# The first product of a PEER layer on 224 tokens, with the expert rows of 32 tokens gathered by index and multiplied on VectorE

## The chip, the cores and the metric

One core of a Trainium2 chip runs the whole program. The metric is the device time of one execution in microseconds. A small part lies around the span that the trace records. Engines are named as in the profile: PE is TensorE (PEld its weight loads), DVE is VectorE, ACT is ScalarE, POOL is GpSimd, SP is SyncE. SP issues the loads of the weights; POOL can issue DMAs too.

## The reference

Two blocks of two layers each work on 256 tokens of width 1024. Only the feed-forward part of the second block's two layers is touched. There every token picks 128 of 16384 experts, 16 for each of 8 heads, by a product-key search:

```python
def peer_ffn(h, w_q, sub_keys, peer_u, peer_v):
    ...
        s = jnp.einsum('thpk,pnk->thpn', q, sub_keys)          # 8 heads, 2 halves, 128 keys
        s_top, i_top = lax.top_k(s, PEER_TOPK)                 # 16 of 128 on each half
        ...
        g_top, pos = lax.top_k(cand, PEER_TOPK)                # 16 of the 256 sums
        expert = jnp.take_along_axis(cand_idx, pos, axis=-1)   # 128 * key1 + key2
        g = jax.nn.softmax(g_top, axis=-1)
        u = jnp.take(peer_u, expert, axis=0)
        act = gelu(jnp.einsum('thkd,td->thk', u, xb))
        vv = jnp.take(peer_v, expert, axis=0)
        return jnp.einsum('thk,thkd->td', g * act, vv)
```

All inputs are FP32, and `peer_u` and `peer_v` are 64 MB a layer each.

## The kernel before, in words

The kernel does not take rows. `peer(l)` runs all 16384 experts as 128 chunks of 128, for all 256 tokens, and lets the weights of a token be zero where an expert was not chosen. A chunk c holds the experts with first key c.

- **A weight block** of 128x1024 is loaded by SP into one of four buffers `raw` (512 KB), rounded by ACT to FP32R (`whi`, L177), and the rest is taken by DVE or POOL (`wlo`, L180). `whi` and `wlo` have five buffers each. `mm3` then makes one FP32 product out of three FP32R matmuls (hi by hi, hi by lo, lo by hi; L185 to L187).
- **up(c)** multiplies a block of `peer_u` by the 256 normed tokens, 8 x 3 matmuls of 256 columns into `pA`, and puts the gelu of it into the row c of `act1` or `act2`. For c below 64 the `wlo` of every third chunk runs on POOL, all others on DVE.
- **Route**: during the chunks 0 to 54 or so, DVE carries out the top-k search as a list of small steps, let in behind the chunks in order.
- **weigh(half, t0)** takes 8 tokens and 64 chunks: DVE builds one-hot matrices in FP16 (`e2`, `e0`, `e1`), 16 small matmuls make the routing weights `pG` from them, and DVE multiplies `act` by `pG` in place (L979).
- **down(c)** rounds the row c of `act` (`wr`), and multiplies it by the block c of `peer_v`, 4 x 3 matmuls of 512 columns into the accumulators `acc`.

The order of the work in a layer: up for c = 0 to 63 with the route; up for 64 to 99 with weigh(0); then 28 chunks with down(c) and up(100+c); down for 28 to 63 with weigh(1); and down for 64 to 127. Instructions are put on each engine's queue by a scheduler that follows the program, the buffers and the holds (`issue_after`); each engine then carries out its own queue strictly in order. In the places below, DVE's queue is what counts: which instruction stands ahead of which.

Of the kernel before, what the change touches and what calls it, by code (L numbers as in the profile page):

```python
# [7 lines left out]
F32 = mybir.dt.float32  # L8
# [8 lines left out]
D = 1024  # L17
# [11 lines left out]
FIRST_HI, FIRST_LO = "aaaa", "vvvv"  # L29

FREE, LAST = 4, 6

AHOLD, HOLD, PACE = 24, 10, 85
NEG = -1e30
# [2 lines left out]
def bc(ap, shape):  # L37
    return ap.to_broadcast(shape)
# [77 lines left out]
class Net:  # L116
# [776 lines left out]
        nc.scalar.copy(dst[0][:, c, :], src)  # L893
        nc.vector.tensor_tensor(dst[1][:, c, :], src, dst[0][:, c, :].bitcast(F32), op=ALU.subtract)

    def peer(self, l, norm, g2, nxt, out=None):
        nc, tc, d = self.nc, self.tc, self.d


        N1, NA, FIN, GATE, TAIL = 64, 100, 58, 110, 4  # L900
        LAG = 128 - NA
        with ExitStack() as ctx:
            P = lambda c, name, bufs=1: c.enter_context(tc.tile_pool(name=f"{name}{l}", bufs=bufs))
            h = norm.h
            wr = self.np.tile([128, 2, 2, S], F32R, tag="xa1", name="wr")
            slots = P(ctx, "pea").tile([128, 4, S], F16, name="slots")
# [6 lines left out]

            def up(c, dst, lo_eng=None):
                w = self.split_w(d["peer_u"][l, c], lo_eng=lo_eng)
                p = self.pa.tile([128, S], F32, tag="sc", name="pA")
                for k in range(KD):
                    mm = self.mm3(p, [v[:, k * 128:(k + 1) * 128] for v in w], [v[:, k, :] for v in h],
                                  k == 0, k == KD - 1)
                return mm, nc.scalar.activation(dst, p, AF.Gelu)  # L920
# [6 lines left out]
            steps, ends = self.route(rctx, l, sc, wI, wP)  # L927
            took = 0
            for c in range(64):
                mark = up(c, act1[:, c, :], nc.gpsimd if c % 3 == 0 else nc.vector)  # L930
                if c % 3:
                    with tc.issue_after(self.last_lo.ins):
                        while took < 1.7 * (c + 1):
                            took += next(steps, 1000)
                if c > FIN and self.bg:
                    if c == FIN + 1:
                        with tc.issue_after(self.last_dma.ins):
                            self.ada_setup("ab")
                    spare()
                if c == FIN:  # L940
                    with tc.issue_after(mark[0].ins), tc.issue_after(mark[1].ins):
                        for end in ends:
                            end()
            assert next(steps, None) is None
            rctx.close()
            mid = ExitStack()
# [7 lines left out]
            def weigh(hf, t0):  # L954

                pg = self.pt.tile([128, 64, 8], F32, tag="tp", name="pG")
                e2 = B.tile([128, 2, 128, 4], F16, tag="e2", name="e2")
                e0 = B.tile([128, 2, 64, 4], F16, tag="e0", name="e0")
                tg = lambda a, n: bc(a.rearrange("p (g t) -> p g t", t=4)[:, :, None, :], [128, 2, n, 4])
                i1, i2 = [wI[:, j, t0:t0 + 8] for j in range(2)]  # L960
                nc.vector.tensor_tensor(e2, bc(self.iota4[:, None], [128, 2, 128, 4]), tg(i2, 128), op=ALU.is_equal)
                nc.vector.tensor_tensor(e0, bc(self.iota4[:, None, hf * 64:hf * 64 + 64], [128, 2, 64, 4]), tg(i1, 64),
                                        op=ALU.is_equal)
                for g in range(2):
                    e1 = B.tile([128, 2, 64, 4], F16, tag="e1", name="e1", bufs=2)
                    w = wP[:, :, t0 + 4 * g:t0 + 4 * g + 4]
                    nc.vector.tensor_tensor(e1, bc(e0[:, g:g + 1], [128, 2, 64, 4]), bc(w[:, :, None, :], [128, 2, 64, 4]),
                                            op=ALU.mult)
                    for t in range(4):
                        for j in range(2):  # L970
                            nc.tensor.matmul(pg[:, :, 4 * g + t], lhsT=e2[:, g, :, t], rhs=e1[:, j, :, t],  # L971
                                             start=(j == 0), stop=(j == 1))
                rows = [(i, (hf * 64 + i) % NA) for i in range(64)]
                cuts = [0] + [i for i in range(1, 64) if rows[i][1] in (0, N1)] + [64]
                for i0, i1 in zip(cuts, cuts[1:]):
                    r0 = rows[i0][1]
                    tl, r0 = (act1, r0) if r0 < N1 else (act2, r0 - N1)
                    v = tl[:, r0:r0 + i1 - i0, t0:t0 + 8]
                    nc.vector.scalar_tensor_tensor(v, pg[:, i0:i1, :], 1.0 / WSCALE, v, op0=ALU.mult, op1=ALU.mult)  # L979

            acc = []

# [23 lines left out]
            done = 0  # L1006
            for c in range(64, NA):
                up(c, row(c), nc.vector)
                while done < 32 and done * (NA - 65) < (c - 63) * 32:
                    weigh(0, 8 * done)  # L1010
                    done += 1
            for c in range(LAG):
                down(c)
                up(NA + c, row(NA + c), nc.vector)
                spare(True)
# [77 lines left out]
    def route(self, ctx, l, sc, wI, wP):  # L1093
# [66 lines left out]
                    nc.vector.tensor_tensor(r, r, wP[:, j, ts_], op=ALU.subtract)  # L1160

        pks = []
        return (u for t in range(NT) for u in start(t)), [lambda t=t: end(t, pks[t]) for t in range(NT)]


def layout(inp):
# [79 lines left out]
    if "peer_u_2" in inp:  # L1246
        cat["norm_ffn_g"] = fm(f("norm_ffn_g_2"))
        cat["peer_wq_a"] = tile_a(f("peer_w_q_2")[:, :, :512])
        cat["peer_wq"] = tile_b(f("peer_w_q_2")[:, :, 512:])
        sk = f("peer_sub_keys_2")  # L1250
        L = sk.shape[0]
        cat["peer_sk"] = np.ascontiguousarray(sk.transpose(0, 3, 1, 2).reshape(L, 128, 256))
        cat["peer_u"] = np.ascontiguousarray(f("peer_u_2").reshape(L, 128, 128, KD, 128).transpose(0, 1, 4, 3, 2)
                                             .reshape(L, 128, 128, D))
        cat["peer_v"] = f("peer_v_2").reshape(L, 128, 128, D)
        cat["c_iota"] = np.broadcast_to(np.arange(128, dtype=np.float32), (128, 128)).copy()
    return cat
# [2 lines left out]
@with_exitstack  # L1260
def body(ctx, tc, d, out):
    net = Net(ctx, tc, d)
    norms = [net.first, Norm(net, ("g_pre_mix", 1))]
    norms[0].all()
    net.ahead = LAST
    gm, gf, ada, later = [], [], [], []

    def setup():
        net.ada_setup("ab", "xa1")
        for l in range(2):  # L1270
            gm.append(net.vec("norm_mix_g", l, KD, net.const, f"gm{l}"))
            gf.append(net.vec("norm_ffn_g", l, KD, net.const, f"gf{l}"))
            a, todo = net.ada_vec("ada", l, 48)
            ada.append(a)
            (later if l else net.bg).extend(todo)
            if l == 0:
                ada.append(None)
                ada[1], todo = net.ada_vec("kv_ada", 0, 16)
                net.bg.extend(todo)
        net.gk = net.vec("kv_norm_g", 0, KD, net.const, "gk")  # L1280

    class Late(Norm):


        def __init__(self, i, col, o):
            super().__init__(net, None, b=col[:, o:o + KD])
            self.i = i

        def prepare(self):
            self.gain = row(self.i)  # L1290
            return super().prepare()

    made = []

    def row(i):
        if i >= len(made):
            if i < 4:
                assert not net.bg, len(net.bg)
                a = ada[0]
                items = [(gm[0], a[:, 8:16]), (None, a[:, 16:24]), (gf[0], a[:, 32:40]), (None, a[:, 40:48])]  # L1300
            else:
                a = ada[1]
                items = [(net.gk, kv[:, 8:16]), (gm[1], a[:, 8:16]), (None, a[:, 16:24]), (gf[1], a[:, 32:40]),
                         (None, a[:, 40:48])]
# [5 lines left out]
    norms += [Late(0, ada[0], 0), Late(2, ada[0], 24), Late(4, kv, 0), Late(7, ada[1], 24)]  # L1310
# [4 lines left out]
    net.peer(0, norms[3], lambda: row(3), norms[4])  # L1315
    assert not net.bg
    net.shared_kv_sb(norms[4], (row(5), ada[1][:, 0:KD]), row(6), norms[5])
    net.peer(1, norms[5], lambda: row(8), None, out)


# [16 lines left out]
```

## Time and profile before

| | us |
|---|---|
| median of three runs | 2896.37 (2888.19 to 2897.91) |
| profiled execution | 2893.22 |
| its span in the trace | 2891.4 |
| granted TensorE clock, mean | 0.996 of full speed |

The three runs spread over 9.7 us, 0.33% of their median. The profiled execution lies 3.15 us below the median, and its span is 1.8 us shorter than its time. The profile's busy times say how long an engine had an instruction in work; its groups by line say what an instruction of one form costs and what the engine waited for ahead of it. The two PEER layers lie at about 1090 to 1720 us and 2090 to 2891 us of the span.

### The profile page before, as it was taken

How to read it: one execution, taken by the hardware profiler on the slowest of the kernel's cores; microseconds unless marked ns; L12 is line 12 of the kernel's file. 1: busy time of each engine (PE TensorE's matmuls, PEld its weight loads, DVE VectorE, ACT ScalarE, POOL GpSimd, SP SyncE). 2: the span in 40 equal slices, each digit the busy share in tenths (PEclk: the TensorE clock that was granted, in tenths of full speed). 3: DMA queues.
4: the chain of work that ended last, by engine and by line, in shares of the span. 5: the costliest groups of instructions: out<-in, count | busy, mean ns of one | idle time of the engine just before them, and what ended most of it. 6: DMA issues, size and time to landing. Idle time of an engine off the chain costs nothing.

```text
span 2891.4 us, 50436 instructions
## 1 busy us (share of the span) xinstructions
PE 2846.0 (98%) x19669; PEld 2575.9 (89%) x19669; DVE 2168.8 (75%) x4178; ACT 1442.9 (50%) x2372; POOL 144.2 (5%) x54
## 2 busy tenths in 40 slices
PE   8999999999999999999999999999999999999999
PEld 7998997999997889989999887877899999988887
DVE  6986766886755859968866997686599787569865
ACT  6645445654545854443344344567544434443454
POOL 0000000000000003320000000000033100000000
PEclk9999999999999999999999999999999999999999
DMA  6485775376666455554687358653455545554564
GB/s 210 135 280 191 265 247 190 111 250 221 235 192 186 161 169 163 173 197 139 196 279 254 117 193 284 217 180 101 146 163 182 170 139 166 186 165 131 186 201 146
DMA packets 153713, 543.42 MB, mean 188 GB/s; under 512 B 20018, under 2 KB 21250, under 8 KB 153346
## 3 DMA queue, kind: packets, MB, share of 16 engines
q1 hardware_dynamic: 153474, 540.20, 57.9%
q8 instruction: 154, 2.52, 0.4%
q14 instruction: 85, 0.70, 0.1%
HBM read 539.04 MB, written 1.09 MB: 187 GB/s over the span
## 4 chain that ended last, share of the span: by engine, by line
PE 86%; DVE 11%; ACT 1%; DMA 1%; issue 1%; SPq 0%; DVEq 0%; ACTq 0%
PE acc L185 8%; PE acc L187 8%; PE acc L186 8%; PE mmB L185 7%; PE mmB L186 7%; PE mmB L187 7%; PE pA L185 5%; PE pA L186 5%; PE pA L187 5%; PE mmA L185 5%; PE mmA L186 5%; PE mmA L187 5%; PE pG L971 4%; DVE wlo L180 3%; PE sc L193 1%
## 5 line engine op out<-in xcount | busy, mean ns | idle before, releaser
L177 ACT CAST whi<-raw 128x1024 fp32r<-128x1024 f32 x893 | 935.8, 1050 | 872.1 <-PE pA L186 358.2
L180 DVE TENSOR_TENSOR wlo<-raw,whi 128x1024 fp32r<-128x1024 f32 x849 | 1049.7, 1241 | 344.3 <-ACT whi L177 341.0
L185 PE MATMUL pA<-hhi,whi 128*128 128x256 f32 x2048 | 586.7, 286 | 10.6 <-ACT act L920 9.5
L186 PE MATMUL pA<-hlo,whi 128*128 128x256 f32 x2048 | 579.8, 283 | 0.0
L187 PE MATMUL pA<-hhi,wlo 128*128 128x256 f32 x2048 | 579.6, 283 | 0.0
L185 PE MATMUL mmB<-hhi,whi 128*128 128x256 f32 x1480 | 422.0, 285 | 0.0
L186 PE MATMUL mmB<-hlo,whi 128*128 128x256 f32 x1480 | 420.2, 284 | 0.0
L187 PE MATMUL mmB<-hhi,wlo 128*128 128x256 f32 x1480 | 419.9, 284 | 0.0
L185 PEld LDWEIGHTS pA<-hhi,whi 128*128 128x128 f32 x2048 | 394.2, 192 | 15.1 <-ACT act L920 11.4
L187 PE MATMUL acc<-whi,wr 128*128 128x512 f32 x1024 | 400.4, 391 | 0.8 <-DVE wr L992 0.5
L186 PE MATMUL acc<-wlo,wr 128*128 128x512 f32 x1024 | 401.0, 392 | 0.0
L186 PEld LDWEIGHTS pA<-hlo,whi 128*128 128x128 f32 x2048 | 393.1, 192 | 2.2
L185 PE MATMUL acc<-whi,wr 128*128 128x512 f32 x1024 | 393.2, 396 | 0.0
L187 PEld LDWEIGHTS pA<-hhi,wlo 128*128 128x128 f32 x2048 | 392.8, 192 | 0.0
L185 PEld LDWEIGHTS mmB<-hhi,whi 128*128 128x128 f32 x1480 | 282.8, 191 | 1.8
L187 PEld LDWEIGHTS mmB<-hhi,wlo 128*128 128x128 f32 x1480 | 282.8, 191 | 0.6
L186 PEld LDWEIGHTS mmB<-hlo,whi 128*128 128x128 f32 x1480 | 282.9, 191 | 0.5
L991 ACT CAST wr<-act 128x256 fp32r<-128x256 f32 x256 | 103.5, 406 | 343.7 <-PE acc L186 338.3
L187 PEld LDWEIGHTS acc<-whi,wr 128*128 128x128 f32 x1024 | 192.3, 188 | 44.9 <-DVE wr L992 4.8
L186 PEld LDWEIGHTS acc<-wlo,wr 128*128 128x128 f32 x1024 | 192.6, 188 | 39.2 <-DVE wlo L180 0.6
L185 PEld LDWEIGHTS acc<-whi,wr 128*128 128x128 f32 x1024 | 193.1, 189 | 35.7
L542 DVE CUSTOM_DVE_ANT_0 adaw<-adaw,cb 128x1024 f32<-128x1024 f32 x112 | 136.8, 1222 | 78.4 <-DMA adaw<-in_ada_w 74.7
(353 smaller groups left out, 4037.4 us busy)
## 6 DMA issues: line engine op xcount, KB each, us to landing
raw<-in_peer_u SPq DMA_DIRECT2D x256, 512.0 KB, 3.8
raw<-in_peer_v SPq DMA_DIRECT2D x256, 512.0 KB, 4.3
adaw<-in_ada_w SPq DMA_DIRECT2D x96, 512.0 KB, 4.5
raw<-in_w_gates SPq DMA_DIRECT2D x80, 512.0 KB, 3.7
raw<-in_w_down SPq DMA_DIRECT2D x44, 512.0 KB, 4.0
raw<-in_w_gate SPq DMA_DIRECT2D x36, 512.0 KB, 3.8
raw<-in_w_up SPq DMA_DIRECT2D x36, 512.0 KB, 3.8
raw<-in_w_qkv SPq DMA_DIRECT2D x24, 512.0 KB, 4.5
```

Source lines behind the costliest of these rows:

```text
L177: (nc.vector.tensor_copy if FIRST_HI[i:i + 1] == "v" else nc.scalar.copy)(hi, raw)
L180: self.last_lo = lo_eng.tensor_tensor(lo, raw, hi.bitcast(F32), op=ALU.subtract)
L185: nc.tensor.matmul(out, lhsT=lhs[0], rhs=rhs[0], start=start, stop=False)
L186: nc.tensor.matmul(out, lhsT=lhs[0], rhs=rhs[1], start=False, stop=False)
L187: return nc.tensor.matmul(out, lhsT=lhs[1], rhs=rhs[0], start=False, stop=stop)
L193: self.nc.tensor.matmul(out, lhsT=lhs[a], rhs=rhs[b], start=start and i == 0, stop=stop and i == 2)
L542: nc.vector.tensor_tensor_reduce(w, w, self.csilu, 1.0, 0.0, op0=ALU.mult, op1=ALU.add, accum_out=col[:, j:j + 1])
L971: nc.tensor.matmul(pg[:, :, 4 * g + t], lhsT=e2[:, g, :, t], rhs=e1[:, j, :, t], start=(j == 0), stop=(j == 1))
L991: nc.scalar.copy(gh, row(c))
```

## The change

32 of the 256 tokens (columns 0 to 31, `TG`) are left out of the up matmuls, which now have 224 columns. For these tokens the expert rows are fetched. In each layer POOL issues 32 indirect DMAs (`gather`, L951). Each brings 128 rows of 4 KB (four of the 128 chosen experts of each of the 32 tokens) into a buffer `ug` that is taken from the same four buffers as `raw`. DVE multiplies each by the token rows `xg`, with the sum along the row (`dot`, L956). In the program, gathers stand behind the chunks 32 to 88 or so, and the dot of each stands two chunks behind it.

Around that: `gather_setup` builds `xg` at chunk 4 (five DMAs by SP, one DVE operation), `gather_places` makes the row numbers at chunk 28, and `gather_end` at chunk 92 takes gelu and weight, transposes, and splits the result into three BF16 parts. In weigh, the four groups of 8 tokens that are gathered come last, use three BF16 parts in place of two FP16 parts, and are put into `act` by ACT instead of being multiplied there by DVE. The first weigh stage has 34 chunks and the stage with down and up 30 (36 and 28 before).

```diff
+TG = 32
+NG = 128 // TG
...
-        N1, NA, FIN, GATE, TAIL = 64, 100, 58, 110, 4
+        N1, NA, FIN, GATE, TAIL = 64, 98, 58, 110, 4
+        G0, G1 = 32, 90
...
             def up(c, dst, lo_eng=None):
                 w = self.split_w(d["peer_u"][l, c], lo_eng=lo_eng)
-                p = self.pa.tile([128, S], F32, tag="sc", name="pA")
+                p = self.pa.tile([128, S - TG], F32, tag="sc", name="pA")
                 for k in range(KD):
-                    mm = self.mm3(p, [v[:, k * 128:(k + 1) * 128] for v in w], [v[:, k, :] for v in h],
+                    mm = self.mm3(p, [v[:, k * 128:(k + 1) * 128] for v in w], [v[:, k, TG:S] for v in h],
...
+            def gather(j):
+                r = self.wraw.tile([128, D], F32, tag="raw", name="ug")
+                nc.gpsimd.indirect_dma_start(out=r, out_offset=None, in_=d["peer_u_rows"],
+                                             in_offset=bass.IndirectOffsetOnAxis(ap=gidx[:, j:j + 1], axis=0))
+                return r
+
+            def dot(j, r):
+                nc.vector.tensor_tensor_reduce(r, r, xg, 1.0, 0.0, op0=ALU.mult, op1=ALU.add,
+                                               accum_out=dots[:, j:j + 1])
...
+            for j in range(TG):
+                turn.setdefault(G0 + j * (G1 - G0) // TG, []).append(j)
+            def gathers(c):
...
+                for j in turn.get(c, ()):
+                    got[j] = gather(j)
+                for j in turn.get(c - 2, ()):
+                    dot(j, got.pop(j))
+                if c == G1 + 2:
+                    gather_end()
...
+                    if own:
+                        nc.scalar.activation(v, pg[:, i0:i1, :], AF.Copy, scale=1.0 / WSCALE)
+                    else:
+                        nc.vector.scalar_tensor_tensor(v, pg[:, i0:i1, :], 1.0 / WSCALE, v, op0=ALU.mult, op1=ALU.mult)
...
-                    weigh(0, 8 * done)
+                    weigh(0, (8 * done + TG) % S)
```

What this does to DVE's queue can be read from the order of the instructions. First DVE in the weigh stage of the first PEER layer, before, between the `wlo` of two chunks:

```order
L180 TENSOR_TENSOR wlo_16079<-raw_16076,whi_16078 128x1024
L967 TENSOR_TENSOR e1_15939<-e0_15936,slots_11703 128x512
L979 SCALAR_TENSOR_TENSOR act1_11707<-pG_15876,act1_11707 128x64x8
L967 TENSOR_TENSOR e1_15949<-e0_15936,slots_11703 128x512
L961 TENSOR_TENSOR e2_15993<-iota4_106,slots_11703 128x1024
L962 TENSOR_TENSOR e0_16052<-iota4_106,slots_11703 128x512
L180 TENSOR_TENSOR wlo_16111<-raw_16108,whi_16110 128x1024
```

The same engine and stage in the changed kernel (line numbers are those of the changed file; L183 is the `wlo`, L956 the dot and the reading of its sum, L1048 and L1063 are L967 and L979 of before):

```order
L183 TENSOR_TENSOR wlo_15442<-raw_15439,whi_15441 128x1024
L956 ISA ug_15648,dots_11705<-ug_15648,xg_12483 128x1024
L956 ISA dots_11705 128x1
L1048 TENSOR_TENSOR e1_15298<-e0_15295,slots_11703 128x512
L1063 SCALAR_TENSOR_TENSOR act1_11711<-pG_15233,act1_11711 128x64x8
L1048 TENSOR_TENSOR e1_15308<-e0_15295,slots_11703 128x512
L1037 TENSOR_TENSOR e2_15353<-iota4_106,slots_11703 128x1024
L1038 TENSOR_TENSOR e0_15415<-iota4_106,slots_11703 128x512
L183 TENSOR_TENSOR wlo_15500<-raw_15497,whi_15499 128x1024
```

The dot of `ug_15648` has come in right behind the `wlo` that reads `raw_15439`, ahead of all the weigh work of that chunk.

POOL's queue in the same stage of the changed kernel holds nothing but gathers (before, POOL had no work in this stage). What each waits for stands in brackets; DVE_49 is the count of DVE's finished instructions, which for `ug_15648` is reached with `wlo_15442`. `ug_15648` has the address of `raw_15439`:

```order
L951 DMA ug_15529<-in_peer_u_rows,gidx_11704 128x1024 [waits DMAHW6_49,DMASW0_49,DVE_49]
L951 DMA ug_15648<-in_peer_u_rows,gidx_11704 128x1024 [waits DMAHW0_49,DMASW1_49,DVE_49]
L951 DMA ug_15767<-in_peer_u_rows,gidx_11704 128x1024 [waits DMAHW2_49,DMASW2_49,DVE_49]
```

So the gather of `ug_15648` can start when `wlo_15442` has ended, and the dot that needs it is DVE's next instruction.

DVE in the stretch between the route and the weigh stage, changed kernel (chunks 55 to 63; L545 belongs to another computation):

```order
L183 TENSOR_TENSOR wlo_14589<-raw_14586,whi_14588 128x1024
L956 ISA ug_14756,dots_11705<-ug_14756,xg_12483 128x1024
L956 ISA dots_11705 128x1
L183 TENSOR_TENSOR wlo_14654<-raw_14651,whi_14653 128x1024
L956 ISA ug_14794,dots_11705<-ug_14794,xg_12483 128x1024
L956 ISA dots_11705 128x1
```

Here too a dot stands right behind the `wlo` that frees its buffer. Of the 32 gathers of a layer this is so for 18. For 7 more, 6 to 20 instructions of the route stand between that `wlo` and the dot. The last 7 take a buffer that a `wlo` of POOL frees. Both layers have the same counts.

## Rows read from the trace of the kernel before

**Rows 1.** The page's first part: busy time, share of span, instructions.
```profile
PE 2846.0 (98%) x19669; PEld 2575.9 (89%) x19669; DVE 2168.8 (75%) x4178; ACT 1442.9 (50%) x2372; POOL 144.2 (5%) x54
```

**Rows 2.** Busy time by stage of the second PEER layer; first column the stretch.
```profile
core 0: us, PE busy (x) PEld busy (x) DVE busy (x) ACT busy (x) POOL busy (x), PEclk, DMA share, GB/s
2095.60:2165.00 69.40, 69.39 (x577) 69.31 (x578) 69.33 (x239) 32.45 (x48) 24.48 (x8) 1.00 0.54 172
2165.00:2251.90 86.90, 84.27 (x698) 83.64 (x697) 86.83 (x253) 38.42 (x58) 27.63 (x10) 1.00 0.51 171
2251.90:2284.60 32.70, 32.64 (x272) 32.38 (x272) 16.27 (x32) 18.79 (x30) 7.21 (x3) 1.00 0.66 209
2284.60:2421.50 136.90, 136.90 (x1378) 135.52 (x1378) 118.22 (x198) 48.84 (x74) 0.00 (x0) 1.00 0.45 139
2421.50:2578.80 157.30, 157.30 (x1010) 143.54 (x1009) 80.50 (x84) 75.21 (x112) 0.00 (x0) 1.00 0.61 187
2578.80:2712.40 133.60, 133.60 (x948) 109.20 (x947) 123.16 (x254) 50.07 (x72) 0.00 (x0) 1.00 0.42 129
```

**Rows 3.** Timeline of PE: start, duration, instruction, in three places.
```profile
1200.10 0.28 PE L187 MATMUL pA<-hhi,wlo 128*128 128x256 f32 x1
1206.58 0.28 PE L187 MATMUL pA<-hhi,wlo 128*128 128x256 f32 x1
...
1292.15 1.16 PE L971 MATMUL pG<-e,e 128*128 128x64 f16 x16
1293.12 0.36 PE L185 MATMUL pA<-hhi,whi 128*128 128x256 f32 x1
...
2859.69 0.39 PE L187 MATMUL acc<-whi,wr 128*128 128x512 f32 x1
2863.99 0.39 PE L185 MATMUL acc<-whi,wr 128*128 128x512 f32 x1
```

**Rows 4.** DVE by form, 2284.6 to 2421.5: busy, mean ns, idle before.
```profile
L180 DVE TENSOR_TENSOR wlo<-raw,whi 128x1024 fp32r<-128x1024 f32 x36 | 43.9, 1218 | 3.4 <-ACT whi L177 3.4
L967 DVE TENSOR_TENSOR e<-e,slots 128x512 f16<-128x512 f16 x64 | 26.9, 420 | 13.0 <-PE pG L971 13.0
```

**Rows 5.** DVE by form, whole program: the other operation that multiplies and sums.
```profile
L542 DVE CUSTOM_DVE_ANT_0 adaw<-adaw,cb 128x1024 f32<-128x1024 f32 x112 | 136.8, 1222 | 78.4 <-DMA adaw<-in_ada_w 74.7 <-DMA adaw<-in_kv_ada_w 3.3
L542 DVE DVE_READ_ACCUMULATOR2_ANT ada_ada<- 128x1 f32 x96 | 7.9, 82 | 0.0
```

**Rows 6.** DMA issues, 2095 to 2421: count, KB, us to landing.
```profile
raw<-in_peer_u SPq DMA_DIRECT2D x95, 512.0 KB, 3.6
```

**Rows 7.** POOL by form, whole program.
```profile
L180 POOL TENSOR_TENSOR wlo<-raw,whi 128x1024 fp32r<-128x1024 f32 x44 | 128.2, 2914 | 788.1 <-ACT whi L177 767.8 <-PE pA L186 13.6 <-PE pA L187 6.7
```

**Rows 8.** DVE by form, 2095 to 2252 (the route).
```profile
L180 DVE TENSOR_TENSOR wlo<-raw,whi 128x1024 fp32r<-128x1024 f32 x35 | 50.0, 1448 | 4.5 <-ACT whi L177 4.5
L1133 DVE TENSOR_TENSOR oh<-oh,fi 128x512 f32<-128x512 f32 x16 | 16.9, 1095 | 0.0
```

**Rows 9.** Timeline of DVE and POOL at one place.
```profile
1206.78 2.40 POOL L180 TENSOR_TENSOR wlo<-raw,whi 128x1024 fp32r<-128x1024 f32 x1 [6.61 <-PE pA L186]
1207.29 2.98 DVE L180 TENSOR_TENSOR wlo<-raw,whi 128x1024 fp32r<-128x1024 f32 x1
```

**Rows 10.** Busy time in short stretches of the first PEER layer.
```profile
1255.00:1257.40 2.40, 0.41 (x4) 0.20 (x2) 0.00 (x0) 0.00 (x0) 0.00 (x0) 1.00 0.96 338
1257.40:1260.00 2.60, 0.00 (x0) 0.00 (x0) 0.56 (x1) 2.08 (x2) 0.00 (x0) 0.50 0.87 348
1260.00:1264.20 4.20, 3.49 (x16) 3.50 (x17) 3.16 (x5) 2.80 (x5) 0.00 (x0) 0.50 0.56 170
1264.20:1270.00 5.80, 5.80 (x50) 5.80 (x49) 1.94 (x3) 2.66 (x4) 2.41 (x1) 1.00 0.80 262
```

**Rows 11.** Timeline of PE: FP32 matmuls outside the PEER layers, x2 passes each.
```profile
1977.06 0.70 PE L825 MATMUL sz<-sqT,skT 64*128 64x256 f32 x2
1977.60 0.38 PE L826 MATMUL sz<-sqT,skT 64*128 64x128 f32 x2
```

More of the change, by code (lines that the diff above doesn't have):

```diff
@@ L904, in peer @@
             h = norm.h
[L905 to L906 removed]
+            EA = P(ctx, "pea")
+            slots = EA.tile([128, 4, S], F16, name="slots")
+            gidx = EA.tile([128, TG], U32, name="gidx")
+            dots = EA.tile([128, TG], F32, name="dots")
+            gw = EA.tile([TG, 2, 128], F32, name="gw")
+            gP = EA.tile([128, 3, TG], BF16, name="gP")
             wI, wP = slots[:, 0:2], slots[:, 2:4]
@@ new lines, in gather_setup, with gather_places @@
+            def gather_setup():
+                xg = self.np.tile([128, D], F32, tag="xa1", name="xg")
+                nc.sync.dma_start(xg, shift)
+                fg = self.wraw.tile([128, D], F32, tag="raw", name="fg")
+                for g in range(NG):
+                    nc.sync.dma_start(fg[g * TG:(g + 1) * TG, :], norm.xa[0][0:TG, :])
+                nc.vector.tensor_tensor(xg, xg, fg, op=ALU.add)
+                return xg
+            def gather_places():
+                e = gw[:, 0].rearrange("p (a b) -> p a b", a=8)
+                nc.vector.scalar_tensor_tensor(e, pks[0][0:TG, 0], 128.0, pks[0][0:TG, 1], op0=ALU.mult, op1=ALU.add)
+                eu = self.np.tile([128, 256], U32, tag="junk", name="eu")[0:TG, 0:128]
+                nc.vector.tensor_scalar(eu, gw[:, 0], float(l * 16384), None, op0=ALU.add)
+                for g in range(NG):
+                    nc.sync.dma_start(gidx[g * TG:(g + 1) * TG, :], eu[:, g * TG:(g + 1) * TG])
@@ new lines, in gather_end @@
+            def gather_end():
+                for g in range(NG):
+                    nc.sync.dma_start(gw[:, 0, g * TG:(g + 1) * TG], dots[g * TG:(g + 1) * TG, :])
+                nc.scalar.activation(gw[:, 0], gw[:, 0], AF.Gelu)
+                nc.vector.tensor_tensor(gw[:, 0], gw[:, 0], gw[:, 1], op=ALU.mult)
+                p = self.pt.tile([128, TG], F32, tag="tp", name="tpg")
+                nc.tensor.transpose(p, gw[:, 0], self.ident[0:TG, 0:TG])
+                r = dots
+                nc.scalar.copy(r, p)
+                for j in range(3):
+                    nc.vector.tensor_copy(gP[:, j], r)
+                    if j < 2:
+                        nc.vector.tensor_tensor(r, r, gP[:, j], op=ALU.subtract)
@@ L925, in spare @@
                     self.pop()
-            steps, ends = self.route(rctx, l, sc, wI, wP)
+            steps, ends, pks = self.route(rctx, l, sc, wI, wP)
             took = 0
+            got = {}
+            turn = {}
+            for j in range(TG):
+                turn.setdefault(G0 + j * (G1 - G0) // TG, []).append(j)
+            def gathers(c):
+                if c == G0 - 4:
+                    assert pks
+                    gather_places()
+                for j in turn.get(c, ()):
[3 more added lines that the diff above has]
+                if c == G1 + 2:
+                    assert not got
+                    gather_end()
             for c in range(64):
@@ L934, in peer @@
                             took += next(steps, 1000)
+                if c == 4:
+                    xg = gather_setup()
+                gathers(c)
                 if c > FIN and self.bg:
@@ L956, in weigh @@
                 pg = self.pt.tile([128, 64, 8], F32, tag="tp", name="pG")
-                e2 = B.tile([128, 2, 128, 4], F16, tag="e2", name="e2")
-                e0 = B.tile([128, 2, 64, 4], F16, tag="e0", name="e0")
+                own = t0 < TG
+                dt = BF16 if own else F16
+                parts = [gP[:, j] for j in range(3)] if own else [wP[:, j] for j in range(2)]
+                e2 = B.tile([128, 2, 128, 4], dt, tag="e2", name="e2")
+                e0 = B.tile([128, 2, 64, 4], dt, tag="e0", name="e0")
                 tg = lambda a, n: bc(a.rearrange("p (g t) -> p g t", t=4)[:, :, None, :], [128, 2, n, 4])
@@ L1162, in route @@
         pks = []
-        return (u for t in range(NT) for u in start(t)), [lambda t=t: end(t, pks[t]) for t in range(NT)]
+        return (u for t in range(NT) for u in start(t)), [lambda t=t: end(t, pks[t]) for t in range(NT)], pks
 def layout(inp):
```

43 lines of the change are left out of this document (26 added, 17 removed).

## The prediction

> **What bounds the kernel now.** I read the page's first part, then the busy time by stage, then single instructions. PE is busy for 98% of the span [rows 1], so at first sight fewer columns in its matmuls must be worth time. The stages say otherwise [rows 2]. The first two stretches, 2095.6 to 2251.9, are the up chunks with the route: there DVE is busy for 69.33 of 69.40 and 86.83 of 86.90 us, so it is DVE that has nothing left. In the weigh stage, 2284.6 to 2421.5, PE is full, and DVE has 118.22 of 136.90 us. That leaves it 0.52 us a chunk (18.7 / 36), and most of the 18.7 is DVE's wait for PE's `pG`, 13.0 us [rows 4]. Only in the short stretch before it (16.27 of 32.70) and in the stage with down and up (80.50 of 157.30) has DVE room. The change takes work from PE and gives work to DVE, almost all of it in the stages where DVE has none to spare.
>
> **What it takes from PE.** 54 matmuls of 256 columns from 1200.10 to 1206.58 make 0.120 us each, and 19 of 512 columns from 2859.69 to 2863.99 make 0.226 us [rows 3], so the 256 columns more cost 0.106 us, 0.415 ns a column. 32 columns less are worth 0.0133 us a matmul, 24 x 0.0133 = 0.32 us a chunk, and 82 us over 2 x 128 chunks, but only where PE sets the pace. The third BF16 part adds one small matmul for each of the 32 tokens in each weigh stage; 16 such matmuls take 0.97 us [rows 3], so 32 x 0.06 = 1.9 us a stage.
>
> **What it gives to DVE.** The dot is the same operation as that of L542, which multiplies and sums two 128x1024 tiles: 1222 ns, and 82 ns to read the sum [rows 5]. 32 x 1.30 = 41.6 us a layer. The setup adds one such operation and a few small ones, 1.6 us. In each weigh stage DVE loses four evictions, and makes eight times three multiplications of 128x256 in place of one of 128x512, which takes 0.42 us [rows 4]; I set the one off against the other, within 2 us.
>
> **What DVE then waits for.** This is the largest term, and the order shows it. A gather takes a buffer of the four that the weight loads use; it can't start until the `wlo` that reads the buffer has ended. For 18 of 32 gathers in each layer the dot stands directly behind that very `wlo` on DVE. So DVE ends the `wlo`, POOL starts the DMA, and DVE has nothing else that it may do until the data have landed: one whole gather, G, is spent idle. Behind the waiting dot stand the next chunk's `wlo` and, in the weigh stage, the `e1` and the evictions; PE waits for all of these. The two chunks between gather and dot in the program's text don't help, since the buffer only comes free at the end of them. For 7 more, 6 to 20 route instructions stand between, some 3.2 us, which is two of the units of work into which the route is cut; L1133 alone is 1.10 us [rows 8]. These wait G - 3.2. For the last 7 a `wlo` of POOL frees the buffer, and DVE waits for a part; I take 2 us, between nothing and G.
>
> No row shows an indirect DMA, and POOL issues none now. From below, G has the landing time of the same 512 KB issued by SP in these stages, 3.6 us [rows 6]. From above I add the longest thing that POOL does here, one `wlo` of 2.9 us [rows 7], for whatever it does to make 128 addresses: 6.5 us. I take 4.5, since it is the same number of bytes in pieces of 4 KB, and nearer to the load. The Trainium skill, "DMA: Bandwidth & Descriptors", section "Anatomy of one DMA — SWDGE (gpsimd) path", gives a fixed 2.0 us plus the bytes at 436 GB/s; for 512 KB that is an estimate of 3.2 us, and by it the sum below would be 3045.
>
> **The sum, for one layer.** I take the second layer's stretches for both.
> - DVE's own work up to chunk 97, before: 69.33 + 86.83 + 16.27 + 118.22 = 290.7 [rows 2], less two `wlo` of 1.22 [rows 4] that now come later, 288.2. With the dots and setup (43.2) 331.4. With the waits 18 x 4.5 + 7 x 1.3 + 7 x 2 = 104 it is 435.4 us.
> - The same chunks before took 86.90 + 69.40 + 32.70 + 136.90 x 34/36 = 318.3. So +117.1. PE needs less than these 435 us: it is then the one that waits.
> - The stage with down and up: before 136.90 x 2/36 + 157.30 = 164.9; after 30 chunks of 157.30 / 28 - 0.32 = 5.30, 158.9. So -6.0. Here DVE has room, and PE's gain is real.
> - Second weigh stage: 133.60 for 36 chunks; two chunks of 12 x 0.226 = 2.7 less, 1.9 of small matmuls more: -3.5.
> - Down to the end: nothing changes.
>
> Together +107.6, twice +215. 2893.2 + 215 = 3108, and the median of the runs lies 3.2 above the profiled execution: I predict 3110.
>
> **Bounds.** One us of G is worth 2 x 25 = 50 us: 3065 at 3.6, 3210 at 6.5. Where DVE and POOL work on `wlo` at once they slow each other: DVE's took 2.98 us beside one of POOL's [rows 9], and 1.45 on average in the route against 1.22 after it [rows 4, 8]. DVE now often stands idle then, which may give back 0.23 x 35 = 8 us on `wlo` and as much on the rest: down to -30, 3035. PE's clock goes up or down with its gaps: PE worked for 0.41 us of 1255.0 to 1257.4 and not at all up to 1260.0, and the granted clock was 0.50 from 1257.4 to 1264.2, then 1.00 [rows 10]; that is 1.2 and 2.4 GHz. After the change PE has gaps of that length at each dot. In the weigh stage a gather comes every 1.8 chunks; DVE then needs 1.8 x 3.28 + 1.3 + 4.5 = 11.7 us and PE 1.8 x (2.57 + 1.8 x 0.97) = 7.8. So PE would become the bound only if the clock were at half for two thirds of the time (11.7 x (1 - x/2) = 7.8); I set it at nothing, and up to 1 us a gather, 64 us, for the range. The Trainium skill, "SBUF — State Buffer", section "SBUF: two separate sides", says that a VectorE operation in a two-port mode keeps GpSimd from writing a DMA's descriptors. If that holds for the route work behind the 7 gathers, none of it covers the wait, and the estimate is 7 x 3.2 x 2 = 45 us more. No row here bears on it. Own range of the forecast: 3030 to 3260.
>
> **Rivals.**
> 1. *Faster: PE sets the pace everywhere.* If the gathers landed while DVE had other work, and DVE kept up, the result would be 2893 - 82 + 2 x 3.8 = 2819. For it speaks PE's 98%. Against it: the route has no DVE time at all, and the weigh stage's 0.52 us a chunk pays for 0.9 us a gather, not even for the dot. It would decide only if the waits vanished and some 40 us of DVE's work a layer with them. 5 in 100.
> 2. *Dots cost only themselves.* No waits, as if the buffers came free early. 15 of the dots fall into the route, with the setup +21 us; the short stretch loses its 9 x 0.32 = 3; the first weigh stage has 13 dots, DVE 118.2 - 2.4 + 16.9 = 132.7 against the 129.3 that the same chunks took, +3; later stages -9.5. That is +11.5 a layer, 2916 in the profile, 2919 for the median. Against it stands the order. 5 in 100.
> 3. *224 columns are slow.* The program has FP32 matmuls in two passes, 0.54 us from one of 256 columns to the next, 0.27 a pass [rows 11], against 0.120 for FP32R. No row has an FP32R matmul of under 256 columns. If these fell to one FP32 pass, 0.236 for 224 columns, each chunk would take 2.8 us more, 715 in all: 3.6 ms. Nothing speaks for it but that gap in the rows. 3 in 100.
>
> The forecast has 87 in 100. The runs before spread over 0.33%, so 0.3% (8.7 us) is about what can be told from no change. Slower has 0.92 (the forecast, rival 3, and rival 2 in the main), the same 0.03 (the rest of rival 2), faster 0.05. The range, 3010 to 3265, leaves out the rivals and a little of the forecast's own tails.
>
> **What would show it.** Right: DVE idle ahead of the dot, released by a DMA `ug<-in_peer_u_rows`, about 80 to 110 us a layer; dots of about 1.3 us; gathers of 3.6 to 6.5 us from issue to landing; `pA` matmuls 0.107 us apart; DVE-bound chunks up to 97 at 4.4 us instead of 3.2; PE's share down to about 89% ((2846 - 82 + 8) / 3110). Wrong: dots that find their data there (rival 1 or 2); a gather of over 7 us, where POOL's work on addresses counts for more than I gave it; a clock at half for most of the stretch; `pA` matmuls over 0.2 us apart (rival 3).

## The result and the profile after

The changed kernel takes 3311.15 us (median of 4 runs, 3307.35 to 3315.24) against 2893.99 us before: a ratio of 1.144, 95% interval 1.142 to 1.147. The direction was forecast, the size was not: +417 us measured, +215 forecast. The profiled execution took 3307.35 us, with a span of 3305.6 us. The page's first part, answering to [rows 1]:

```profile
PE 2950.8 (89%) x19799; PEld 2652.0 (80%) x19799; DVE 2229.0 (67%) x4368; ACT 1444.9 (44%) x2400; POOL 204.4 (6%) x118
```

PE fell from 98% to 89%, and no engine took its place: DVE fell too, from 75% to 67%, ACT from 50% to 44%, and POOL stands at 6%. A kernel that gets longer while the shares of its busy engines fall has got waits, not work. The busy time by stage shows where. First the second PEER layer, whose stretches answer to [rows 2]: route (chunks 0 to 54), the short stretch, first weigh stage, down and up, second weigh stage.

```profile
2383.80:2595.30 211.50, 167.73 (x1320) 165.23 (x1320) 170.31 (x526) 71.91 (x110) 67.98 (x34) 0.89 0.53 172
2595.30:2641.30 46.00, 30.87 (x222) 30.48 (x223) 19.84 (x39) 15.94 (x26) 11.22 (x8) 0.78 0.51 170
2641.30:2833.50 192.20, 150.83 (x1364) 147.37 (x1364) 127.89 (x240) 47.69 (x76) 10.31 (x11) 0.87 0.42 129
2833.50:2995.90 162.40, 162.40 (x1083) 148.00 (x1082) 86.34 (x90) 79.89 (x120) 0.00 (x0) 1.00 0.63 195
2995.90:3126.80 130.90, 130.90 (x954) 105.74 (x953) 120.82 (x258) 49.78 (x76) 0.00 (x0) 1.00 0.40 124
```

Up to the first down the layer takes 449.7 us, against 435.4 forecast. DVE's own work in it is 318.0 us (170.31 + 19.84 + 127.89). Of the 131.7 us that are left, 122.5 are waits for gathers, which the forecast named. DVE's waits in the weigh stage (total, times, longest):

```profile
DVE ug L956 <- DMA ug<-in_peer_u_rows,gidx: 57.3, 12, 5.5
DVE e L1045 <- PE pG L1052: 6.2, 5, 1.8
```

12 dots wait 4.8 us each. One of them in the timelines of DVE and POOL, in the order of time:

```profile
2663.73 1.22 DVE L183 TENSOR_TENSOR wlo<-raw,whi 128x1024 fp32r<-128x1024 f32 x1
...
2665.22 0.94 POOL L951 DMA_INDIRECT ug<-in_peer_u_rows,gidx  x1 [12.24 <-DVE wlo L183]
...
2669.55 1.23 DVE L956 CUSTOM_DVE_ANT_0 ug<-ug,xg 128x1024 f32<-128x1024 f32 x1 [4.59 <-DMA ug<-in_peer_u_rows,gidx]
```

The `wlo` ends at 2664.95, POOL starts the gather 0.27 us later, and DVE does nothing until 2669.55. Over the whole program the gathers land 4.4 us (median) after their issue, 4.0 at the least:

```profile
L951 POOL DMA_INDIRECT ug<-in_peer_u_rows,gidx x64: 936/938/2952, 1177.0 to 2762.5; - x64
DMA to landing us min/median/max: 4.0/4.4/6.3
```

The second layer's total thus lies near the forecast. The first one's does not. Its stage with down and up, after and before:

```profile
1576.80:1875.00 298.20, 211.70 (x1083) 179.09 (x1082) 112.45 (x151) 79.25 (x120) 0.00 (x0) 0.83 0.46 150
```
```profile
1426.10:1583.50 157.40, 157.40 (x1010) 143.66 (x1009) 109.06 (x145) 75.33 (x112) 0.00 (x0) 1.00 0.81 271
```

9.9 us a chunk in place of 5.6, with no gather and no dot in the stage. DVE has little to do there (112 of 298 us), and its waits are of one kind:

```profile
DVE adaw L545 <- DMA adaw<-in_ada_w: 183.8, 27, 7.8
DVE wlo L183 <- ACT whi L180: 2.0, 2, 1.2
```

In this layer a background computation goes along with the stage: for each chunk SP loads a third block of 512 KB, `adaw`, and DVE multiplies and sums it (L545, L542 before). Its rows in the changed kernel, SP and DVE in the order of time:

```profile
1682.51 0.33 SPq L169 DMA_DIRECT2D raw<-in_peer_v  x1
...
1682.74 1.22 DVE L183 TENSOR_TENSOR wlo<-raw,whi 128x1024 fp32r<-128x1024 f32 x1
...
1683.98 0.33 SPq L169 DMA_DIRECT2D raw<-in_peer_u  x1
1684.36 0.43 SPq L544 DMA_DIRECT2D adaw<-in_ada_w  x1
...
1689.64 1.23 DVE L545 CUSTOM_DVE_ANT_0 adaw<-adaw,cb 128x1024 f32<-128x1024 f32 x1 [5.68 <-DMA adaw<-in_ada_w]
```

and before:

```profile
1485.00 0.33 SPq L541 DMA_DIRECT2D adaw<-in_ada_w  x1
...
1485.32 1.22 DVE L180 TENSOR_TENSOR wlo<-raw,whi 128x1024 fp32r<-128x1024 f32 x1
1486.46 0.42 DVE L992 TENSOR_TENSOR wr<-act,wr 128x256 fp32r<-128x256 f32 x1
...
1486.80 1.22 DVE L180 TENSOR_TENSOR wlo<-raw,whi 128x1024 fp32r<-128x1024 f32 x1
...
1489.26 1.23 DVE L542 CUSTOM_DVE_ANT_0 adaw<-adaw,cb 128x1024 f32<-128x1024 f32 x1 [1.24 <-DMA adaw<-in_ada_w]
```

The order of the two queues says why. Before, the load of `adaw_17139` stands on SP behind `raw_17107`, which takes the buffer that `wlo_16999` frees; between that `wlo` and the product DVE has another product and two more `wlo` (the numbers tell the buffers apart; these lists show the order of the queues, not times):

```
DVE  wlo_16999, adaw_17084, wlo_17037, wr, wlo_17055, adaw_17139, wlo_17092, wr, wlo_17110<-raw_17107
SP   raw_17107, adaw_17139
```

After, the product stands two `wlo` earlier. `raw_17230` takes the buffer that `wlo_17122` frees, and DVE's next instruction is the product that needs the load behind it:

```
DVE  wlo_17122, adaw_17262, wlo_17160, wr, wlo_17178, adaw_17317, wlo_17215, wr, wlo_17233<-raw_17230
SP   raw_17230, adaw_17262
```

The trace before adds one thing. There the load most often waited for the product ahead of it, which frees its own buffer: at 1485.00 SP issues it just as the product that began at 1483.74 has ended. SP's wait for that, and DVE's wait for the load, in this stage of the kernel before:

```profile
SPq L541 <- DVE ada_ada L542: 50.9, 21, 3.6
DVE adaw L542 <- DMA adaw<-in_ada_w: 37.4, 23, 2.7
```

So before, two `wlo` and a `wr` (2.7 us) stand between the start of the load and the product, and cover most of it. After, nothing does: the `wlo` ends at 1683.96, SP issues the weight load and then the `adaw` load, DVE waits until it has landed, and only then come the `wlo` that free the next buffers: a ring that takes 10 us to go round once. It is the pattern of the gathers, in a stage where nobody had put a gather, and it can be read from the order of the two kernels ahead of any run.

### The profile page after: what moved, and what is told of

It reads as the page before. It is cut to its first block, busy times and chain, and to the rows that moved or that the text cites. A ratio compares the mean times of both kernels' runs of the same rounds, so it can differ in the third digit from the quotient of the medians.

```text
span 3305.6 us, 51219 instructions
## 1 busy us (share of the span) xinstructions
PE 2950.8 (89%) x19799; PEld 2652.0 (80%) x19799; DVE 2229.0 (67%) x4368; ACT 1444.9 (44%) x2400; POOL 204.4 (6%) x118
## 5 line engine op out<-in xcount | busy, mean ns | idle before, releaser
L183 DVE TENSOR_TENSOR wlo<-raw,whi 128x1024 fp32r<-128x1024 f32 x849 | 1040.1, 1229 | 301.8 <-ACT whi L180 298.3
L188 PE MATMUL pA<-hhi,whi 128*128 128x224 f32 x2048 | 605.4, 296 | 113.2 <-ACT act L929 112.1
L189 PE MATMUL pA<-hlo,whi 128*128 128x224 f32 x2048 | 595.5, 291 | 0.0
L190 PE MATMUL pA<-hhi,wlo 128*128 128x224 f32 x2048 | 593.5, 290 | 1.2 <-DVE wlo L183 1.2
L188 PEld LDWEIGHTS pA<-hhi,whi 128*128 128x128 f32 x2048 | 430.8, 210 | 122.2 <-ACT act L929 117.5
L189 PEld LDWEIGHTS pA<-hlo,whi 128*128 128x128 f32 x2048 | 428.0, 209 | 7.8 <-issue 4.9
L190 PEld LDWEIGHTS pA<-hhi,wlo 128*128 128x128 f32 x2048 | 426.4, 208 | 1.6 <-DVE wlo L183 1.4
L190 PE MATMUL acc<-whi,wr 128*128 128x512 f32 x1024 | 417.7, 408 | 1.0 <-DVE wr L1076 1.0
L188 PE MATMUL acc<-whi,wr 128*128 128x512 f32 x1024 | 407.2, 409 | 0.0
L545 DVE CUSTOM_DVE_ANT_0 adaw<-adaw,cb 128x1024 f32<-128x1024 f32 x112 | 137.1, 1224 | 269.9 <-DMA adaw<-in_ada_w 253.5
L189 PEld LDWEIGHTS acc<-wlo,wr 128*128 128x128 f32 x1024 | 201.4, 197 | 136.7 <-DVE wlo L183 95.1
L1052 PE MATMUL pG<-e,e 128*128 128x64 f16 (+1 forms) x2176 | 179.0, 255 | 94.1 <-DVE e L1048 81.8
L1052 PEld LDWEIGHTS <-e 128*128 128x128 f16 (+1 forms) x2176 | 147.6, 125 | 117.0 <-issue 91.0
L190 PEld LDWEIGHTS acc<-whi,wr 128*128 128x128 f32 x1024 | 201.6, 197 | 48.1 <-DVE wr L1076 4.7
```

The costliest lines, as they stand in the source:

```text
L183: self.last_lo = lo_eng.tensor_tensor(lo, raw, hi.bitcast(F32), op=ALU.subtract)
L188: nc.tensor.matmul(out, lhsT=lhs[0], rhs=rhs[0], start=start, stop=False)
L189: nc.tensor.matmul(out, lhsT=lhs[0], rhs=rhs[1], start=False, stop=False)
L190: return nc.tensor.matmul(out, lhsT=lhs[1], rhs=rhs[0], start=False, stop=stop)
L545: nc.vector.tensor_tensor_reduce(w, w, self.csilu, 1.0, 0.0, op0=ALU.mult, op1=ALU.add, accum_out=col[:, j:j + 1])
```

## The experiments

The theory that came out of this: the time is lost in DVE's order, where an instruction that needs a load stands directly behind the one that lets the load start, at two places (dots, and `adaw` products). The rivals put it down to the gathers and dots themselves (DVE's work, the shared buffers, the DMAs).

**Only the `adaw` products held back.** The hold is `issue_after`, which the kernel uses for other steps already; it puts an instruction behind another one in the order. Here that is the last `wlo` of the chunk.

```diff
-            nc.vector.tensor_tensor_reduce(w, w, self.csilu, 1.0, 0.0, op0=ALU.mult, op1=ALU.add,
-                                           accum_out=col[:, j:j + 1])
+            with self.tc.issue_after(self.ada_gate) if self.ada_gate else ExitStack():
+                nc.vector.tensor_tensor_reduce(w, w, self.csilu, 1.0, 0.0, op0=ALU.mult, op1=ALU.add,
+                                               accum_out=col[:, j:j + 1])
...
                 up(NA + c, row(NA + c), nc.vector)
+                self.ada_gate = self.last_lo.ins
                 spare(True)
+                self.ada_gate = None
```

> The changed kernel, but in the first layer's stage with down and up DVE's product on each ada weight block (L545) is held behind the wlo of the chunk, as it stood before the change; the gathers and dots stay as they are. Theory (order): in that stage the product stands ahead of two wlo more than before, so DVE waits out a whole ada load in each chunk and the weight loads behind it start late; held back, the stage takes 30 x 5.4 = 162 to 170 us in place of 298, and the whole 3311 - 133 = about 3178. Rival (load): three loads of 512 KB a chunk cannot arrive faster after the change; the stage stays at 10 us a chunk and the time at 3311.

Measured 3161.92 us, ratio 1.094 (1.092 to 1.096): 149 us back, 136 of them in the stage and 12 in the first layer's chunks ahead of it. The stage:

```profile
1565.30:1727.70 162.40, 162.40 (x1082) 147.97 (x1081) 113.72 (x153) 78.27 (x120) 0.00 (x0) 1.00 0.83 277
```

It takes what the second layer's takes, with PE full and 277 GB/s loaded. The load was not the limit; the order was.

**Only the dots held back.**

```diff
                 for j in turn.get(c - 2, ()):
-                    dot(j, got.pop(j))
+                    with tc.issue_after(self.last_lo.ins):
+                        dot(j, got.pop(j))
```

> The changed kernel, but each dot is held behind the wlo of the chunk behind which the program has it, so that 6 to 20 us of other DVE work stand between the wlo that frees the gather's buffer and the dot in most cases; the ada products stay as in the changed kernel. Theory (order): DVE's 234 us of idle time ahead of the dots nearly vanish, the chunks up to 97 take about 345 us a layer in place of 484 and 450, and the whole 3311 - 245 = about 3065. Rival (gathers as such: they take a buffer from the weight loads, and POOL's descriptor work stands in DVE's way): less than half of that comes back, above 3190.

Measured 3188.34 us, ratio 1.103 (1.101 to 1.105). DVE's wait for gathers fell from 234 us (201.4 put down to the DMA, 32.3 to issue) to 42.9, but only 123 us came back. That is half of the theory's 245, and the time lies within 2 us of where the rival begins. Nearly all of it came back in the chunks 55 to 97, where dots stand directly behind the `wlo` that frees their buffer: the second layer's weigh stage fell from 192.2 to 144.2 us. In the chunks 32 to 54 the hold gained next to nothing (122.0 and 111.8 us in the two layers, 125.7 and 110.7 without it). DVE's waits there, second layer, with the hold:

```profile
DVE wlo L183 <- ACT whi L180: 16.6, 5, 5.0
DVE ug L956 <- DMA ug<-in_peer_u_rows,gidx: 15.7, 3, 5.4
```

Together they are as long as the 33.8 us without it: what a dot no longer waits for, a `wlo` waits for.

**Both.**

> Both holds together. Theory (order): the two losses are separate and add, 3311 - 133 - 245 = about 2930, that is the dots' own time in the route, less what 224 columns give in the stages where PE sets the pace. If 224 columns and a free queue made the change a gain, it would come out under 2885. Rival (gathers as such): above 3050.

Measured 3042.86 us, ratio 1.053 (1.051 to 1.054). The two losses do add: 149 + 123 = 272, and 268 came back. But 154 us more than before remain, and the result lies 7 us from the rival's 3050 and 113 from the theory's 2930: order alone does not explain it. In the second layer's chunks 0 to 54 DVE waits for this (total, times, longest):

```profile
DVE wlo L183 <- ACT whi L180: 22.9, 8, 5.0
DVE ug L957 <- DMA ug<-in_peer_u_rows,gidx: 16.2, 3, 5.6
```

and ACT, in turn, for the weight loads:

```profile
ACT whi L180 <- DMA raw<-in_peer_u: 92.3, 20, 9.2
```

**All 256 columns again.** The 32 tokens' columns are computed and not used; nothing is held.

```diff
-                p = self.pa.tile([128, S - TG], F32, tag="sc", name="pA")
+                p = self.pa.tile([128, S], F32, tag="sc", name="pA")
...
-                    mm = self.mm3(p, [v[:, k * 128:(k + 1) * 128] for v in w], [v[:, k, TG:S] for v in h],
+                    mm = self.mm3(p, [v[:, k * 128:(k + 1) * 128] for v in w], [v[:, k, :] for v in h],
...
-                return mm, nc.scalar.activation(dst[:, TG:S], p, AF.Gelu)
+                return mm, nc.scalar.activation(dst[:, TG:S], p[:, TG:S], AF.Gelu)
```

> The changed kernel with up matmuls over all 256 columns again (the 32 gathered tokens are computed and not used), gathers and dots as they are, no hold. In this program's order the dots stand 6 to 25 us of DVE work behind the wlo that frees their buffer, and the ada products where they stood before the change. Theory (order): although each chunk has more to multiply, it is faster than the changed kernel by some 360 us: before plus the dots in the route (15 x 1.3) and the first weigh stage, about 24 a layer, 2945. Rival (dots and gathers cost by themselves): slower than the changed kernel by the columns, 3311 + 50.

Measured 3004.06 us, ratio 1.039 (1.037 to 1.042). With more to multiply the kernel is 307 us faster than the changed one. In this program's order dots and products stand elsewhere, and DVE's waits for gathers fall from 233.7 to 44.3 us, those for `ada_w` loads from 253.5 to 84.4. Here, too, 60 us more remain than expected.

**What remains, split.** The gathers and dots left out (the sums set to zero, so that the 32 tokens get nothing from their experts), with the hold on the products:

> The changed kernel without its gathers and dots (the sums are set to zero, so the 32 tokens get nothing from their experts), with 224 columns, setup, weigh and end as they are, and with the hold on the ada products. It shows what leaving the columns out is worth by itself. By the matmul pitch of the changed kernel's rows (0.111 us for 224 columns against 0.120) 24 x 0.009 = 0.21 us a chunk over some 73 chunks a layer in which PE sets the pace, less small matmuls and the wait in the end of the gathering: nothing that can be told, 2890 within 15. Rival (the prediction's 0.32 us a chunk, and the route too): 2845 or less.

Measured 2925.7 us, ratio 1.012 (1.010 to 1.013): the theory's range is missed by 21 us on the slow side, and the rival lies the other way. What is left of the change (224 columns, setup, end, three BF16 parts, other chunk counts) costs 34 us. The chunks 0 to 31 take 104.5 us in the first layer here and 104.6 in the second, with DVE idle for 9 us in each. With the gathers, but no dots:

> The same with the 64 gathers back (into the four buffers of the weight loads, read by nobody) but no dots, and the hold on the ada products. It splits what is left in the run with both holds, 3043 against 2889. Theory A (buffers: with a gather in one or two of four, weight loads come late, and DVE waits for ACT's whi): 2950 or more. Theory B (the dots' own DVE time and what waits remain before them): 2915 or less.

Measured 2975.64 us, ratio 1.029 (1.027 to 1.031). Theory A's range holds it: gathers that nobody reads cost 50 us. DVE's wait in the second layer's chunks 0 to 63, with these gathers and without them:

```profile
DVE wlo L183 <- ACT whi L180: 50.6, 16, 7.5
```
```profile
DVE wlo L183 <- ACT whi L180: 24.5, 10, 7.5
```

What SP's weight loads waited for in the second layer names the buffer, once for each of the 32 gathers:

```profile
SPq L169 <- DMA ug<-in_peer_u_rows,gidx: 183.1, 32, 10.3
```

A gather in one of four buffers delays the weight loads. That the gathers' traffic slows the loads is the other reading. No run parts the two; but in the second layer's chunks 32 to 63 a `peer_u` load lands in 3.8 us with both holds and in 3.7 without gathers (medians), which speaks for the buffer. The dots on top of that cost 67 us (3042.86 - 2975.64), less than their own time, 64 x 1.3 = 83.

**One buffer for the gathers alone**, without and with the hold on the dots; the products are held in both. The first weigh stage has 30 chunks here, and the stage with down and up 34.

```diff
-        N1, NA, FIN, GATE, TAIL = 64, 98, 58, 110, 4
+        N1, NA, FIN, GATE, TAIL = 64, 94, 58, 110, 4
...
-        G0, G1 = 32, 90
+        G0, G1 = 32, 86
...
+            UG = P(ctx, "pug")
...
-                r = self.wraw.tile([128, D], F32, tag="raw", name="ug")
+                r = UG.tile([128, D], F32, name="ug")
```

> The changed kernel with one buffer for the gathers alone (4 KB a partition, made free by a first weigh stage of 30 chunks in place of 34; gathers behind chunks 32 to 85), and the hold on the ada products. The weight loads have their four buffers again. But in this program's order most dots stand directly behind the dot before them, which frees that one buffer. Theory (order: what counts is DVE's work between the instruction that frees the buffer and the dot): no better than the run with the ada hold alone, 3160 within 50. Rival (sharing the weight buffers is the cause): below 3050.

Measured 3235.13 us, ratio 1.119 (1.116 to 1.121), 25 us above the range of the theory and far from the rival. The waits for gathers are about those of the changed kernel (233.7 us):

```profile
DVE ug L958 <- DMA ug<-in_peer_u_rows,gidx: 244.3, 62, 7.9
```

An own buffer does not take the wait away: what stands between its release and the dot does. The run gives no price for the buffer, because the order moved with it: all gathers are issued ahead of chunk 55 here, the second layer's last at 2549.9, while the chunk's first up matmul starts at 2595.7.

> The same with the dots held behind the wlo of their chunk as well. Now 1 to 13 us of other work stand between two dots, most often 4 or more, and the weight loads have four buffers. Theory A of the run without dots (buffers): it regains most of what the run with both holds still loses to late weight loads, 2960 to 3005. Theory B: about as the run with both holds, 3030 or more.

Measured 3091.96 us, ratio 1.069 (1.067 to 1.071): theory A's number is missed, and the result lies in the range of theory B. But the run decides less than it was meant to: with one buffer, 29 dots still wait, 100.8 us together. It says that one own buffer is not enough, and nothing on two.

**Only the columns.** The kernel before with 224 columns in the up matmuls (the 32 rows of `act` set to zero once) and nothing else, without and with the hold on the products:

> The kernel before with one edit: the up matmuls have 224 columns (the 32 tokens' rows of act are set to zero once, so they get nothing from their experts). No gathers, no setup, no other chunk counts, weigh as before. In this program's order the ada products of the first layer stand two wlo earlier than before, as in the changed kernel. Theory (order): the 28 chunks of that stage take 10 us each, 280 in place of 157, and the columns give 0.21 us x 73 chunks x 2 = 31 back: 2892 + 123 - 31 = about 2984, slower than before although it only does less. Rival (the loss in that stage has to do with gathers or with the longer stage): 2861.

Measured 3033.32 us, ratio 1.050 (1.048 to 1.052): a kernel that multiplies less, and has no gather, is 142 us slower. That is 49 more than the theory's 2984. The first layer's stage with down and up, and what DVE waited for in it:

```profile
1452.40:1732.90 280.50, 198.31 (x1009) 167.70 (x1010) 108.04 (x146) 75.33 (x115) 0.00 (x0) 0.83 0.46 151
DVE adaw L544 <- DMA adaw<-in_ada_w: 170.2, 25, 7.6
```

> The same with the hold on the ada products. Theory: what leaving the columns out is worth at most, 2892 - 31 = about 2861; by the prediction's 0.32 us a chunk it would be 2845, and if the route gained too 2810.

Measured 2887.42 us, ratio 0.9988 (0.9978 to 0.9998). The hold alone is worth 146 us here, and none of the three expected numbers is met. Leaving out an eighth of the columns of the up product is worth 4 us of 2891, at the edge of what can be told. In each layer the first weigh stage (130.1 us against 136.9, from its first up matmul to the first down) and the stage with down and up (151.6 against 157.4) get 12.6 us shorter together; the chunks 0 to 63 give it back, 208.6 and 193.2 us against 195.6 and 189.0.

**The control of the hold**, in the kernel before.

> The kernel before with the hold on the ada products alone, as a control of the hold: there PE sets the pace of the stage, so nothing moves: 2892 within 9. If the hold by itself made the kernel faster, the runs with it would have to be read against this one.

Measured 2893.52 us, ratio 1.0006 (0.9996 to 1.0016): the hold does nothing to the kernel before.

**The setup on POOL**, with both holds.

```diff
-                nc.vector.tensor_tensor(xg, xg, fg, op=ALU.add)
+                nc.gpsimd.tensor_tensor(xg, xg, fg, op=ALU.add)
```

> Both holds, and the addition in the setup (xg, L939) on POOL in place of DVE. In all runs with the setup SP issues no weight load for 12.5 us, until that addition has read the buffer fg that it took from the weight loads; DVE comes to it only after a dozen route steps. Theory (setup): POOL does it at once, and the first 32 chunks of each layer get about 8 us shorter: 3043 - 16 = about 3027. Rival (those 8 us are DVE's or PE's work, not the load's wait): 3043 within 5.

Measured 3034.38 us, ratio 1.050 (1.048 to 1.052); 8 of 16 us, half of what was expected, and outside the rival's range too. The gap on SP, from one weight load's issue to the next, is there still, 12.3 us, and it is 12.8 in the kernel with the columns alone, which has no setup, and 9.7 in the kernel before. SP's wait in it, 12.3 us for the addition with both holds, is now 12.1 us for a step of the route. So the addition was not the only thing that held the gap open, and the theory on the setup falls. Where the 8 us came from is not shown.

## Why the prediction was wrong

The runs make a ladder, each rung one part more (the kernel before, measured anew beside them, had medians of 2889 to 2894 us). A rung's size holds for this order of adding the parts:

| | us | step |
|---|---|---|
| before | 2891 | |
| 224 columns, products held | 2887 | -4 |
| and setup, end, BF16 parts, chunk counts | 2926 | +38 |
| and gathers in the weight buffers | 2976 | +50 |
| and dots, held | 3043 | +67 |
| dots where the program's order has them | 3162 | +119 |
| products where the order has them: the changed kernel | 3311 | +149 |

- **The step that failed** is the third of the sum: "The stage with down and up: before 136.90 x 2/36 + 157.30 = 164.9; after 30 chunks of 157.30 / 28 - 0.32 = 5.30, 158.9. So -6.0. Here DVE has room, and PE's gain is real." For the second layer that is nearly right, 162.4. For the first it was 298.2, 139 us more, and this is most of the 199 us by which the profiled execution's rise (3305.6 - 2891.4 = 414 in the span) passed 215. The first layer's chunks ahead of the stage make another 42, the second layer 14 + 4. "I take the second layer's stretches for both" hid it: the first layer has a third load per chunk, with a product on DVE that can be late. "DVE has room" was right as a share (112 of 298 us busy), and a share does not say whether DVE waits; the wait was put at nothing, though [rows 5] had 74.7 us of it before this very product. The run with the hold, in which the stage takes 162.4 us, shows that the order of this product is the cause there; the columns alone, with and without the hold, show that the 224 columns bring the order about without any gather. Why the scheduler puts it there is not shown.
- **DVE's waits for the gathers** were seen rightly in place, and in size where the dot stands behind the `wlo`: G was taken as 4.5, and the gathers land 4.4 us after issue, with 4.8 us of wait per dot in the weigh stage. They came to 122.5 us in the second layer (3.2 + 1.5 in chunks 0 to 31, 33.8 in 32 to 54, 26.7 and 57.3 after) against 104. The 17 dots after chunk 54 have 84.0 of it, where the sum had 81 for 18; the 15 ahead of it have 38.5, where the sum had 23 for 14, so the route covers less of a gather than it was given. The bound of 3.6 from the SP load was too low by 0.8, that of 6.5 too high by 2.1.
- **DVE's own work** was put at 331.4 us and measured at 318.0. The sum has 13.4 too much here, 18.5 too little in the waits for gathers, and lacks 9.2 of other idle time. These partly cancel: that the second layer's total, 449.7 against 435.4, is only 14.3 off is in part luck.
- **The first layer's chunks up to the first down** took 484.0 us, where the second's took 449.7. They rose by 159 us, 42 more than the 117 of the sum. 30.8 us are waits for `adaw` loads (8.6, 13.5 and 8.7 in three stretches), of which the kernel before had 8.4; the rest was not followed up.
- **The setup** was put at 1.6 us a layer, all of it DVE's work. In the run without gathers the chunks 0 to 31 take 104.5 and 104.6 us, and 93.7 and 94.7 with the columns alone, held: 21 of the 38 us of that rung lie there. DVE is idle for 9 us of them in each layer, and for 0.1 with the columns alone. What makes it wait is open.
- **The column price** was too high: 224 columns run at 0.111 us (from 2928.24 to 2930.35, 19 steps), not 0.107. That is 0.21 us a chunk in place of 0.32.
- **The clock** was set at nothing, and the rows leave it little: the granted clock fell to 0.87 in the weigh stage, but DVE's work and its waits for gathers fill 185.2 of its 192.2 us (127.9 + 57.3).
- **Rival 1** (PE sets the pace) is refuted by the columns alone, held: even without any gather the 82 us are not there. **Rival 2** (dots cost only themselves, 2919) falls with the 233.7 us of waits for gathers in the changed kernel; and with most of them gone, in the run with both holds, gathers in the weight buffers still cost 50 us, and the small parts 38. **Rival 3** (slow 224 columns) falls with the pitch of 0.111 us.
- Of the two rules of the Trainium skill: "DMA: Bandwidth & Descriptors", "Anatomy of one DMA — SWDGE (gpsimd) path", gives an estimate of 3.2 us for 512 KB. The trace does not agree: 4.0 us at the least, 4.4 in the median, with other loads under way; the measurement decides. The other, "SBUF — State Buffer", "SBUF: two separate sides", has a VectorE operation in a two-port mode keep GpSimd from writing descriptors. With both holds, where DVE works during most gathers, they land after 5.1 us in the median and not 4.4. This agrees in sign, but weight loads run at the same time, no row tells which operations are in that mode, and no run parts the two.

No version came out that beats the kernel before. An estimate from the runs says why that is hard: with the columns alone 12.6 us a layer are won in the stages that PE fills, and the dots alone are 41.6 us of DVE's time.

## What to carry to other kernels

Read the order on the waiting engine for every load, not only for the new ones: find the instruction that frees a load's buffer, or that of the load ahead of it in the queue, and count the work that stands between it and the instruction that needs the data. Where there is none, the whole transfer is a wait, each time round. And a smaller operation is not harmless to a program whose order a scheduler makes: 32 columns less in the matmuls of PE moved a product on DVE that has nothing to do with them, and cost 142 us until that product was held in its place.

## What was not expected of the hardware

A gather of 128 rows of 4 KB, issued by POOL, lands only 0.6 us later than a plain load of the same size by SP: 4.4 us against 3.8 for the `peer_u` loads of the same stretch in the second layer. The prediction had allowed for 2.9 us more. POOL is busy for 0.94 us with a gather in the median, and for 2.95 at most.
